# Experts' tokens by row gathers from HBM instead of selection matmuls, in a one-core hybrid layer with a mixture of experts

## Chip, cores and metric

The kernel runs on one core of a Trainium2 chip. The metric is the device time of one execution in microseconds (us).

## What is computed

One layer over 512 latent tokens of width 1024: modulated RMSNorm, two parallel branches (retention and a gated long convolution) merged and projected by `w_out`, a gated residual, and then the part that matters here: a second modulated RMSNorm, a two-level router and 32 SwiGLU experts, of which each token takes two.

```python
x = x + gt1 * mix                                  # mix ends with "@ w_out"
h2 = rms_norm(x, norm2_g) * (1 + sc2) + sh2        # u, the experts' input
group_p = softmax(u @ rg_w + rg_b)                 # 4 groups, the best one
in_group = (u @ re_w + re_b) of that group         # 8 experts, the best two
weights = p_star * w_top / sum(w_top)
for each expert e: y = (silu(x_e @ w1[e]) * (x_e @ w3[e])) @ w2[e]   # x_e: the tokens that chose e
x = x + gt2 * (sum over a token's two experts of weight * y)
return rms_norm(x, final_norm_g)
```

Everything is fp32. An expert has 6.3 MB of weights, all experts together 201.3 MB, and each is read once.

## The kernel before, in words

The first half of the program (up to about 548 us) computes the two branches and their merge; the change leaves it as it is. Behind it come four stages.

*W_out* (`out_group`, `fm_products`, line 1279 on). The product with `w_out` is made feature-major: for each of two halves, eight k-steps of twelve matmuls (weight and activation are each split into a high and a low fp32r part, `mm3`). `out_tile` (line 1236) turns each of eight finished 128x512 tiles into the residual `xm` by one DVE instruction, and makes two copies of it: `xa`, scaled by the modulation `am2c` (1 + sc2 times the norm's gain), and `sq2`, its square.

*Router* (`router_step`, `tail`, lines 1252 to 1340). For each of the eight feature tiles one matmul of `rw` against `xa` and one of ones against `sq2` run over all 512 tokens as moving columns. The result `rl` lies feature-major and is turned to token-major by way of `rsum`. Four of the eight steps run between the steps of the second half of W_out, four behind them. Meanwhile `xa` is turned to token-major, split into `h2H` and `h2L`, and kept in SBUF. After the norm's scale `mrs` come two rounds of a top search (`top`, line 1370), and `pos` (line 1403): for each token and each of 32 experts the token's place in the expert's list (1 to 64, or 0).

*Choice of the experts' tokens* (`select_steps`, line 1444). Four experts make a group, two a pair, and each expert has 64 slots (`CAP`). For a group, DVE builds the 0/1 matrix `gtm` (512 tokens by 256 slots) by comparing `slots` with `pos`. PE then makes the experts' columns `xgm` (features by slots) by multiplying: for each of eight feature tiles, 4 token tiles by two parts of `h2`, so 64 matmuls of 256 columns (lines 1466 and 1467). Another eight (`rss`, line 1457) bring the norm's scale to the slots; DVE multiplies by it, ACT adds the shift `sh2c`.

*Experts* (loop at line 1629). For a pair: `up_half` (16 + 16 matmuls by w1 and w3, two experts side by side in the array), `hidden` (SiLU, product), `turned` (four PE transposes), `down` (by w2), and `add`, which scatters the results back to the tokens by the turned choice `cmb` and adds them to `xmid`, the token-major residual. `spread` (line 1474) makes `cmb` and the slots' weights `wsl`. PE's order is as written in the loop (`manual_schedule` for PE); the stage from `tail` to the first expert's columns is written out for all engines; elsewhere the scheduler orders.

*Weights.* 192 tiles of 1 MB (`plan`, line 1168) come over SP's DMA queue in the order in which they are used, issued ahead by `ahead` (line 1211). Tiles live in a ring of `NR` = 10 places; beside it, places are lent (`loans`, line 1190): for four tiles at the start those of `y`, `cmb`, `hh` and `hT`, later two in every 13 tiles those of `xm` and one (`XE`) those of `xe0` and `xe1`. A tile is issued only when its place is free. The pool `wk`, in which the lent places lie, overlays the tiles of the first half (`wide`), `xa`, `sq2` and W_out's operands among them. One overflow branch (`OV` = pair 10) treats experts with more than 64 tokens; with these inputs it isn't entered.

```python
1465            for t in range(4):
1466                T.matmul(p, h2[0][:, t, ks], gt[:, t], start=(t == 0), stop=False)
1467                T.matmul(p, h2[1][:, t, ks], gt[:, t], start=False, stop=(t == 3))
1468            x_ = x4[:, k % 4]
1469            V.tensor_tensor(out=x_, in0=p, in1=rss, op=ALU.mult)
1470            A.activation(x_, x_, AF.Identity, bias=sh2c[:, k:k + 1])
```

Of the kernel before, what the change touches and what calls it, by code (L numbers as in the profile page):

```python
# [31 lines left out]
NA, NB, NC, NR, NW, NH = 12, 33, 4, 10, 2, 3  # L32
# [5 lines left out]
XE = 8  # L38
# [10 lines left out]
W = 4, 2, 1, 6, 2  # L49
# [124 lines left out]
def body(es: ExitStack, tc: tile.TileContext, d, out, dump=None):  # L174
# [890 lines left out]
    def rest_of_modulation():  # L1065
# [37 lines left out]
        V.scalar_tensor_tensor(out=am2c, in0=am2c, scalar=1.0, in1=n2, op0=ALU.add, op1=ALU.mult)  # L1103
        yield
# [58 lines left out]
    h2 = [r2.tile([128, 4, 1024], F32R, name="h2%s" % n) for n in "HL"]  # L1163
# [18 lines left out]
    def borrow(pool, tag, bufs, units):  # L1182
        def tile_():
# [13 lines left out]
                 if (i - early_tiles) % (NR + 3) < 2 and not 12 * OV + 8 <= i < 12 * OV + 8 + OA + 8)  # L1197
    loans.update((i, [borrow(wk_, "xe0", 1, 2), borrow(lambda: late, "xe1", 1, 2)]) for i in range(early_tiles, len(plan) - 4)
                 if (i - early_tiles) % (NR + 3) == XE)
# [33 lines left out]
    xa, sq2 = [None] * 8, [None] * 8  # L1233
    rl = []

    def out_tile(o, k):
        xk = xm[k // 2][:, k % 2, :]
        V.scalar_tensor_tensor(out=xk, in0=o, scalar=gt1c[:, k:k + 1], in1=xk, op0=ALU.mult, op1=ALU.add)
        if k % 2 == 0:
            xw = wide("xa", (128, 2, 512))  # L1240
            sw = wide("sq2", (128, 2, 512))
            xa[k], xa[k + 1], sq2[k], sq2[k + 1] = xw[:, 0, :], xw[:, 1, :], sw[:, 0, :], sw[:, 1, :]
        if k >= 4 and k % 2:
            V.tensor_scalar(out=xa[k], in0=xk, scalar1=am2c[:, k:k + 1], scalar2=None, op0=ALU.mult)
        else:
            A.activation(xa[k], xk, AF.Copy, scale=am2c[:, k:k + 1])
        A.activation(sq2[k], xk, AF.Square)
# [9 lines left out]
    def turned_tokens(t, n, tag):  # L1257

        p = bank("h2t", tag)
        for q in range(4):  # L1260
            T.transpose(p[:, 128 * q:128 * q + 128], xa[4 * n + q][:, 128 * t:128 * t + 128], ident)
        return [h[:, t, 512 * n:512 * n + 512] for h in h2] + [p]

    def early_steps():
        rl.append(bank("rl"))
        yield
        for k in range(4):
            router_step(k)
            yield
        for t in range(4):  # L1270
            split(*turned_tokens(t, 0, "x"))
            yield
# [25 lines left out]

    tri, ones_b = (rk(n, [128, 128], dt=BF16) for n in ("tri", "ones_b"))
# [8 lines left out]

    def tail():

        for m in range(4):
# [4 lines left out]
            if m > 1:  # L1316
                router_step(2 + m)
        router_step(6)
        router_step(7)
        early_table(AF.Sqrt, sq2[7][:, 0:1])  # L1320
        tk = [turned_tokens(t, 1, "acc") for t in range(2)]
        rsum = wide("rsum")[0:96, 0:512]
        V.tensor_copy(rsum, rl[0][0:96])
        A.copy(tk[0][0], tk[0][2])
        p = bank("lt")
        for t in range(4):
            T.transpose(p[:, 96 * t:96 * t + 96], rsum[:, 128 * t:128 * t + 128], ident[0:96, 0:96])
        pv = p[:, 0:384].rearrange("p (t e) -> p t e", t=4)
        tk += [turned_tokens(t, 1, "acc") for t in range(2, 4)]

        def low(t):
            V.tensor_tensor(out=tk[t][1], in0=tk[t][2], in1=f(tk[t][0]), op=ALU.subtract)

        rsqrt_mean(mrs, pv[:, :, 64], 1024, mtmp, mss)
        for t in range(1, 4):
            A.copy(tk[t][0], tk[t][2])
        V.tensor_tensor(out=lgt, in0=pv[:, :, 0:40], in1=mrs[:, :, None].to_broadcast([128, 4, 40]), op=ALU.mult)
        V.tensor_tensor(out=lgt, in0=lgt, in1=lconst[:, None, :].to_broadcast([128, 4, 40]), op=ALU.add)
        dump("lgt", lgt)
        return tk, low  # L1340
# [3 lines left out]
    tk, low = tail()  # L1344

# [4 lines left out]
    rsb = wk.tile([128, 2, 4], F32R, name="rsb")  # L1350
    xmid = wk.tile([128, 4, 1024], F32, name="xmid")

    def residual():
        for t in range(4):
            for n in range(2):
                p = bank("xmt")
                for q in range(4):
                    k = 4 * n + q
                    T.transpose(p[:, 128 * q:128 * q + 128], xm[k // 2][:, k % 2, 128 * t:128 * t + 128], ident)
                A.copy(xmid[:, t, 512 * n:512 * n + 512], p)  # L1360
                if t == 1 and n:
                    A.copy(rsb[:, 0], mrs)
            dump("xm_%d" % t, xmid[:, t, :])

    def b8(t):
        return t[:, :, :, None].to_broadcast([128, 4, 5, 8])

# [12 lines left out]
    residual()  # L1380
# [18 lines left out]
    V.tensor_tensor(out=rsb[:, 1], in0=mrs, in1=f(rsb[:, 0]), op=ALU.subtract)  # L1399
    low(0)  # L1400
# [6 lines left out]
    def shares():  # L1407
# [7 lines left out]
        for u, oh in ((v1, oh1), (v2, oh2)):  # L1415
            V.tensor_tensor(out=oh, in0=oh, in1=e, op=ALU.mult)
            V.tensor_reduce(out=u, in_=oh, axis=AX.X, op=ALU.add)
        gw = rk("gw", [128, 4, 4])
# [9 lines left out]
        A.copy(wHL[:, :, :, 0, :], wtv)  # L1428
        V.tensor_tensor(out=wHL[:, :, :, 1, :], in0=wtv, in1=f(wHL[:, :, :, 0, :]), op=ALU.subtract)
# [9 lines left out]

# [364 lines left out]
```

## Time and profile before

| | |
|---|---|
| time, median of 3 runs (lowest to highest) | 1124.71 us (1123.62 to 1126.41) |
| the profiled execution: time, span | 1124.28 us, 1122.6 us |
| busy: PE, DVE, ACT, POOL | 98%, 52%, 31%, 2% |
| moved by DMA | 283.22 MB, mean 252 GB/s |
| of it SP's queue, POOL's queue | 274.51 MB, 7.80 MB |
| first expert product (start) | 625.63 us |

The time is that of the whole execution, the span runs from the first to the last instruction on the core; 1.7 us lie around it. Busy shares are means over stages with different limits, and a matmul that waits in the pipeline counts as busy, so the stages are read one by one. In the rows, L12 is line 12 of the kernel before; engines are PE (matmul), PEld (its weight load), DVE, ACT, POOL, SP; a name with q is an engine's queue, on which DMAs are issued.

### The profile page before, as it was taken

How to read it: one execution, taken by the hardware profiler on the slowest of the kernel's cores; microseconds unless marked ns; L12 is line 12 of the kernel's file. 1: busy time of each engine (PE TensorE's matmuls, PEld its weight loads, DVE VectorE, ACT ScalarE, POOL GpSimd, SP SyncE). 2: the span in 40 equal slices, each digit the busy share in tenths (PEclk: the TensorE clock that was granted, in tenths of full speed). 3: DMA queues.
4: the chain of work that ended last, by engine and by line, in shares of the span. 5: the costliest groups of instructions: out<-in, count | busy, mean ns of one | idle time of the engine just before them, and what ended most of it. 6: DMA issues, size and time to landing. Idle time of an engine off the chain costs nothing. (4 is left out here: it accounts for less than half of the span.)

```text
span 1122.6 us, 13708 instructions
## 1 busy us (share of the span) xinstructions
PE 1100.6 (98%) x5338; PEld 710.5 (63%) x5338; DVE 582.1 (52%) x1041; ACT 349.4 (31%) x620; POOL 18.6 (2%) x41
## 2 busy tenths in 40 slices
PE   6999999999999999999999999999999999999996
PEld 3667888877778777877865644454545454645443
DVE  1788995765475768965524523333333323332333
ACT  2487352435533554333234311020202010201113
POOL 0010000000000000000000000000000000000000
PEclk8999999999999999999999999999999999999999
DMA  7653343211122118874392978999999998999992
GB/s 271 209 172 109 112 136 126 75 57 57 57 86 64 57 38 286 263 265 160 129 415 94 398 303 358 417 416 418 415 418 416 419 417 350 399 415 417 418 381 76
DMA packets 63135, 283.22 MB, mean 252 GB/s; under 512 B 6806, under 2 KB 8982, under 8 KB 44506
## 3 DMA queue, kind: packets, MB, share of 16 engines
q1 hardware_dynamic: 60970, 274.51, 64.2%
q0 software_dynamic: 2096, 7.80, 2.1%
q8 instruction: 43, 0.70, 0.3%
q14 instruction: 26, 0.21, 0.1%
HBM read 280.18 MB, written 2.10 MB: 251 GB/s over the span
## 5 line engine op out<-in xcount | busy, mean ns | idle before, releaser
L198 DVE TENSOR_TENSOR wL<-raw,wH 128x512 fp32r<-128x512 f32 x142 | 97.2, 688 | 120.0 <-ACT wH L197 111.3
L197 ACT CAST wH<-raw 128x512 fp32r<-128x512 f32 x142 | 88.1, 621 | 213.3 <-PE ro L202 33.7
L1498 PE MATMUL ga<-ew,xgm 128*64 128x512 f32 x416 | 108.2, 593 | 0.0
L1504 DVE TENSOR_TENSOR hh<-hh,up 128x512 f32<-128x512 f32 x16 | 11.0, 688 | 176.4 <-PE up L1498 176.4
L1498 PE MATMUL up<-ew,xgm 128*64 128x512 f32 x376 | 100.9, 592 | 0.0
L1523 PE MATMUL y<-ew,hT 128*64 128x512 f32 x368 | 97.7, 606 | 1.6 <-DVE hT L1512 1.1
L197 ACT CAST yh<-yv 128x512 fp32r<-128x512 f32 x30 | 18.5, 618 | 200.5 <-DVE yv L1529 187.1
L1498 PEld LDWEIGHTS ga<-ew,xgm 128*64 128x64 f32 x416 | 34.3, 137 | 57.9 <-issue 54.9
L1498 PEld LDWEIGHTS up<-ew,xgm 128*64 128x64 f32 x376 | 31.9, 137 | 54.3 <-issue 52.9
L1523 PEld LDWEIGHTS y<-ew,hT 128*64 128x64 f32 x368 | 30.1, 139 | 48.2 <-issue 46.2
L1466 PE MATMUL xg<-gtm,h2H 128*128 128x256 f32 x256 | 60.5, 280 | 0.0
L1467 PE MATMUL xg<-gtm,h2L 128*128 128x256 f32 x256 | 59.8, 278 | 0.0
L1529 DVE SCALAR_TENSOR_TENSOR yv<-y,wsl,gt 128x512 f32<-128x512 f32 x30 | 22.4, 748 | 62.2 <-PE y L1523 53.1
L1503 ACT ACTIVATE hh<-ga 128x512 f32<-128x512 f32 x16 | 9.6, 597 | 132.2 <-PE ga L1498 129.9
L1466 PEld LDWEIGHTS xg<-gtm,h2H 128*128 128x128 f32 x256 | 48.1, 188 | 0.8 <-issue 0.8
L1467 PEld LDWEIGHTS xg<-gtm,h2L 128*128 128x128 f32 x256 | 48.1, 188 | 0.0
L1546 DVE TENSOR_TENSOR xmid<-xmid,co 128x512 f32<-128x512 f32 x58 | 39.8, 687 | 12.5 <-PE co L1538 11.9
L1538 PE MATMUL co<-yh,cmb 128*128 128x512 f32 x114 | 46.1, 404 | 0.0
L1469 DVE TENSOR_TENSOR xgm<-xg,rss 128x256 f32<-128x256 f32 x64 | 27.0, 424 | 35.3 <-PE xg L1467 35.3
L1538 PE MATMUL co<-yl,cmb 128*128 128x512 f32 x114 | 44.7, 392 | 0.0
L1470 ACT ACTIVATE xgm<-xgm,sh2c 128x256 f32<-128x256 f32 x64 | 32.4, 509 | 35.7 <-DVE xgm L1469 35.7
L342 DVE SCALAR_TENSOR_TENSOR acc<-adaw,scT,acc 128x1024 f32<-128x1024 f32 x28 | 35.6, 1282 | 10.8 <-DMA adaw<-ada 10.7
(478 smaller groups left out, 2383.7 us busy)
## 6 DMA issues: line engine op xcount, KB each, us to landing
ew<-w SPq DMA_DIRECT2D x148, 1024.0 KB, 13.2
raw<-w_in SPq DMA_DIRECT2D x52, 512.0 KB, 3.9
xwxm<-w SPq DMA_DIRECT2D x52, 512.0 KB, 15.0
adaw<-ada SPq DMA_DIRECT2D x32, 512.0 KB, 5.9
xwxe<-w SPq DMA_DIRECT2D x26, 512.0 KB, 16.5
adaw<-ada SPq DMA_DIRECT2D x32, 256.0 KB, 6.2
raw<-ret_w_o SPq DMA_DIRECT2D x8, 512.0 KB, 3.7
raw<-w_out SPq DMA_DIRECT2D x8, 512.0 KB, 4.0
```

The costliest lines, as they stand in the source:

```text
L197: A.copy(h, src)
L198: V.tensor_tensor(out=l, in0=src, in1=f(h), op=ALU.subtract)
L342: V.scalar_tensor_tensor(out=acc[i], in0=w, scalar=scT[:, k, 0:1], in1=acc[i], op0=ALU.mult, op1=ALU.add)
L1466: T.matmul(p, h2[0][:, t, ks], gt[:, t], start=(t == 0), stop=False)
L1467: T.matmul(p, h2[1][:, t, ks], gt[:, t], start=False, stop=(t == 3))
L1469: V.tensor_tensor(out=x_, in0=p, in1=rss, op=ALU.mult)
L1470: A.activation(x_, x_, AF.Identity, bias=sh2c[:, k:k + 1])
L1498: T.matmul(ab_[i][64 * e:64 * e + 64], xg[k][:, c0 + 64 * e:c0 + 64 * e + 64], w[e][q], start=(k == 0), stop=(k == 7))
L1523: T.matmul(y_[n][64 * e:64 * e + 64], hT_[:, 128 * k + 64 * e:128 * k + 64 * e + 64], w[e][2 * q + n], start=(k == 0), stop=(k == 3))
L1529: V.scalar_tensor_tensor(out=yv, in0=y_[n], scalar=wsl, in1=gt2[:, ns], op0=ALU.mult, op1=ALU.mult)
L1538: T.matmul(p, cmb[:, 128 * t:128 * t + 128], y[j][:, ns], start=(start and i + j == 0), stop=(i == len(parts) - 1 and j == 1))
L1546: V.tensor_tensor(out=xmid[:, t, ns], in0=xmid[:, t, ns], in1=p, op=ALU.add)
```

## The change

The experts' columns are no longer made by a product with the choice. Each token's residual row is copied to HBM (`rows`, 512 x 1024) by eight POOL DMAs as soon as it is turned to token-major. For a pair of experts the matmul that gave the slots' weights (`slot_sums`) now also sums, for each slot, the norm's scale (two parts) and the token's number minus 1024. `fetched` adds 1024 to that sum, which gives an index, and issues an indirect DMA on POOL's queue that reads row `idx` of `rows` into the slot's partition of `xr`; an empty slot's index is 1024, beyond the bound of 511. `scaled` multiplies the row by the norm's scale (half on DVE, half on ACT), `token_columns` turns it by eight PE transposes, and DVE and ACT apply `am2c` and `sh2c` as they move the turned columns to `xgm`. `xr` has one buffer for each pair of a group.

The modulation goes into the router's weights (`rw` times `am2c`), so `xa` and `h2` are gone. The router is token-major: `xm` is the stationary side and 40 columns of `rw` move, so no turn of its result is needed; it runs in three partial sums. The squares are added up on DVE and summed by eight one-column products. `xmid` is made in the router's stage rather than by `residual` behind it. The ring has 12 places rather than 10, and `xf` is one more place to lend. In the expert loop, the choice of the next group is made during the group's first pair, and `described` (slot sums, gathers, weights, turned choice) stands behind `add` and ahead of the first pair's `down`.

```diff
-NA, NB, NC, NR, NW, NH = 12, 33, 4, 10, 2, 3
+NA, NB, NC, NR, NW, NH = 12, 33, 4, 12, 2, 3
-XE = 8
+XE, XF = 8, 12
-W = 4, 2, 1, 6, 2
+W = 4, 2, 1, 10, 2, 8
...
+        V.tensor_tensor(out=rw, in0=rw, in1=am2c[:, :, None].to_broadcast([128, 8, 64]), op=ALU.mult)
...
+    loans.update((i, [borrow(wk_, "xf", 1, 4)]) for i in range(early_tiles, len(plan) - 4)
+                 if (i - early_tiles) % (NR + 4) == XF)
...
-    def router_step(k):
-
-        T.matmul(rl[0][0:64], rw[:, k, :], xa[k], start=(k == 0), stop=(k == 7))
-        T.matmul(rl[0][64:96], ones[:, 0:32], sq2[k], start=(k == 0), stop=(k == 7))
+    def router_part(ks, t):
+        p = rl[-1][:, 40 * t:40 * t + 40]
+        for k in ks:
+            T.matmul(p, xk_tile(k, t), rw[:, k, 0:40], start=(k == ks[0]), stop=(k == ks[-1]))
...
+    def kept(t, n, p):
+        ns = slice(512 * n, 512 * n + 512)
+        A.copy(xmid[:, t, ns], p)
+        G.dma_start(rows[128 * t:128 * t + 128, ns], xmid[:, t, ns])
...
-    def select_steps(pos, n, name, res, slots, tag="xg", bufs=2):
...
+    def slot_sums(gt, c0, whl):
+        p = bank("wsl")
+        n = whl.shape[-1]
         for t in range(4):
+            T.matmul(p[:, 8 - n:8], gt[:, t, c0:c0 + 128], whl[:, t], start=(t == 0), stop=(t == 3))
+        return p
+
+    def fetched(p, j):
+
+        idx = wk.tile([128, 1], I32, name="idx", tag="idx", bufs=2)
+        rs = wk.tile([128, 1], F32, name="rs", tag="rs", bufs=2)
+        V.tensor_scalar(out=idx, in0=p[:, 6:7], scalar1=1024.0, scalar2=None, op0=ALU.add)
+        G.indirect_dma_start(out=xr[j], out_offset=None, in_=rows,
+                             in_offset=bass.IndirectOffsetOnAxis(ap=idx, axis=0), bounds_check=511, oob_is_err=False)
+        V.tensor_reduce(out=rs, in_=p[:, 4:6], axis=AX.X, op=ALU.add)
+        return rs
+
+    def scaled(rs, j):
+        V.tensor_scalar(out=xr[j][:, 0:512], in0=xr[j][:, 0:512], scalar1=rs, scalar2=None, op0=ALU.mult)
+        A.activation(xr[j][:, 512:1024], xr[j][:, 512:1024], AF.Copy, scale=rs)
...
+            for j, pr in enumerate(pairs):
+                T.transpose(p[:, i + 128 * j:i + 128 * j + 128], xr[pr][:, 128 * k:128 * k + 128], ident)
...
+            if k % 2:
+                A.activation(o, p[:, i:i + w], AF.Identity, bias=sh2c[:, k:k + 1], scale=am2c[:, k:k + 1])
+            else:
+                V.tensor_scalar(out=o, in0=p[:, i:i + w], scalar1=am2c[:, k:k + 1], scalar2=sh2c[:, k:k + 1],
+                                op0=ALU.mult, op1=ALU.add)
...
+            if g < 7:
+                nxt = described(g + 1, gt)
...
-        hh = up(a + 1, sel[1])
+        hh = up(a + 1, xg)
         if g < 7:
-            some(more, 3)
+            for j in range(2):
+                scaled(rs[j], j)
             hT_ = turned(hh)
-            run(more)
-            spr = [spread(nxt[0], 128 * j, weights_of(a + 2 + j)) for j in range(2)]
+            xg = column_tiles(4, "m")
+            token_columns(xg, [0, 1])
             parts.append((now[1][0], down(hT_, now[1][1], ahead_weights)))
```

The order in which the instructions stand shows three places. The first is SP's queue from the last load of `w_out` on, where the weight tiles are issued ahead (`ew` is the ring; `xwy`, `xwcmb`, `xwxm`, `xwxe` and `xwxf` are lent places, and four rows of 128x512 or two of 128x1024 make one tile). Before:

```order
L484 DMA raw<-w_out 128x1024
L1225 DMA ew<-w 128x2048 x5
L1207 DMA xwy<-w 128x1024 x4
L1207 DMA xwcmb<-w 128x512 x4
L1207 DMA xwhh<-w 128x512 x2
L1207 DMA xwhT<-w 128x512 x2
```

The changed kernel, at the same place (the lines are those of its own text):

```order
L484 DMA raw<-w_out 128x1024
L1230 DMA ew<-w 128x2048 x7
L1212 DMA xwy<-w 128x1024 x4
L1212 DMA xwcmb<-w 128x512 x4
L1212 DMA xwhh<-w 128x512 x2
L1212 DMA xwhT<-w 128x512 x2
L1212 DMA xwxm<-w 128x1024 x4
L1212 DMA xwxe_5353<-w 128x1024
L1212 DMA xwxf<-w 128x2048
```

Two more ring tiles stand ahead of the first lent place, and a lent tile `xwxf` is new; the order of the rest is kept.

The second place is POOL's queue from the start of the expert stage's constants to the second group. Before, it holds a broadcast only:

```order
L830 TENSOR_TENSOR sq<-sq 128x512 x3
L1307 IOTA slots 128x64
L1607 ISA
L1607 ISA gt_5263<-mrow_70 128x512 x2
L1560 TENSOR_LOAD nrounds
L1561 COMPARE_AND_BRANCH
```

The changed kernel:

```order
L1322 IOTA slots 128x64
L1273 DMA rows<-xmid 128x512 x8
L1376 MEMSET xr_5098 128x1024
L1376 MEMSET xr_5099 128x1024
L1483 DMA xr_5098<-rows,idx 128x1024
L1483 DMA xr_5099<-rows,idx 128x1024
L1648 ISA
L1648 ISA gt_5274<-mrow_70 128x512 x2
```

The row copies and the clearing of `xr` stand ahead of the first two gathers, and the broadcast of `gt2` behind them; later groups have two gathers each.

The third place is DVE in a middle group of the changed kernel, from the four additions to `xmid` that end a group's first pair to its first `yv`. Before, `yv` followed the additions directly:

```order
L1546 TENSOR_TENSOR xmid<-xmid,co 128x512 x4
L1512 COPY hT<-hT 128x512
L1546 TENSOR_TENSOR xmid<-xmid,co 128x512 x4
L1529 SCALAR_TENSOR_TENSOR yv<-y,wsl,gt_5263 128x512
L198 TENSOR_TENSOR yl<-yv,yh 128x512
L1529 SCALAR_TENSOR_TENSOR yv<-y,wsl,gt_5263 128x512
L198 TENSOR_TENSOR yl<-yv,yh 128x512
```

The changed kernel:

```order
L1582 TENSOR_TENSOR xmid<-xmid,co 128x512 x4
L1482 TENSOR_SCALAR idx<-wsl 128x1
L1485 TENSOR_REDUCE rs<-wsl 128x1
L1524 TENSOR_REDUCE wsl<-wsl 64x1 x2
L1517 CAST cmb<-cmb 128x512
...
L1466 TENSOR_TENSOR gtm<-slots,pos 128x4x128 x2
L1489 TENSOR_SCALAR xr_5098<-xr_5098,rs 128x512
L1489 TENSOR_SCALAR xr_5099<-xr_5099,rs 128x512
L1565 SCALAR_TENSOR_TENSOR yv<-y,wsl,gt_5274 128x512
```

The two scalings of `xr`, which need the gathered rows, now stand ahead of `yv` on DVE.

## Rows read from the trace of the kernel before

**Rows 1.** The page: the span, and each engine's busy time, share and instructions.
```profile
span 1122.6 us, 13708 instructions
...
PE 1100.6 (98%) x5338; PEld 710.5 (63%) x5338; DVE 582.1 (52%) x1041; ACT 349.4 (31%) x620; POOL 18.6 (2%) x41
```

**Rows 2.** Windows: stretch, length, busy per engine, PE clock, DMA share, GB/s.
```profile
595.00:613.00 18.00, 18.00 (x81) 9.64 (x80) 8.26 (x15) 8.67 (x16) 1.48 (x2) 1.00 0.00 1
613.00:650.00 37.00, 35.90 (x235) 23.29 (x235) 21.50 (x66) 12.86 (x25) 0.00 (x0) 0.96 0.95 369
650.00:690.00 40.00, 40.00 (x228) 20.18 (x226) 13.63 (x28) 7.52 (x14) 0.00 (x0) 0.99 0.81 310
690.00:925.00 235.00, 235.00 (x1258) 120.16 (x1256) 77.44 (x144) 31.24 (x58) 0.00 (x0) 1.00 1.02 417
925.00:965.00 40.00, 39.48 (x184) 17.65 (x182) 13.93 (x23) 3.07 (x5) 0.00 (x0) 1.00 0.92 357
...
1095.00:1112.00 17.00, 17.00 (x67) 8.40 (x66) 5.03 (x11) 4.10 (x12) 0.00 (x0) 1.00 0.00 1
```

**Rows 3.** SP's timeline (start, length) and its waits (total, times, longest us).
```profile
574.31 2.35 SPq L1225 DMA_DIRECT2D ew<-w  x5
612.89 1.75 SPq L1207 DMA_DIRECT2D xwy<-w  x4
...
SPq L1207 <- DVE xa L1244: 29.8, 1, 29.8
```

**Rows 4.** The chain that ended last, one group: start, us, engine, instructions.
```profile
949.72 7.13 PE y L1523 x32
...
970.58 1.13 PE rss L1457 x8
971.71 0.12 PE xg L1466
...
973.60 0.44 PE hT L1510 x4
...
979.70 0.44 PE cmb L1479 x4
...
1010.05 7.02 PE y L1523 x32
```

**Rows 5.** PE's timeline: a router step, W_out's last product, the first expert product.
```profile
575.35 1.07 PE L1254 MATMUL rl<-xa,rw 128*64 128x512 f32 x2
...
577.33 0.50 PE L201 MATMUL wo<-mixed,wH 128*128 128x512 f32 x1
...
604.26 0.40 PE L203 MATMUL wo<-mixed,wL 128*128 128x512 f32 x1
...
625.63 3.65 PE L1498 MATMUL ga<-ew,xgm 128*64 128x512 f32 x16
```

**Rows 6.** DMA: a queue's share of 16 engines; issues (count, KB each, us to landing).
```profile
q0 software_dynamic: 2096, 7.80, 2.1%
...
ci<-dft_i POOLq DMA_DIRECT2D x4, 512.0 KB, 3.7
...
xwxe<-w SPq DMA_DIRECT2D x26, 512.0 KB, 16.5
```

**Rows 7.** DVE's timeline: the first search of the router, and `pos`.
```profile
613.94 0.32 DVE L1373 TENSOR_REDUCE t1v<-lgt 128x20 f32<-128x160 f32 x1
...
619.55 0.29 DVE L1403 SCALAR_TENSOR_TENSOR pos<-cum,asg 128x128 f32<-128x128 f32 x1 [0.39 <-PE cum L1398]
```

**Rows 8.** PE's timeline: the first pair's y products behind an idle microsecond.
```profile
647.20 5.35 PE L1523 MATMUL y<-ew,hT 128*64 128x512 f32 x16 [1.08 <-DVE hT L1512]
652.38 3.60 PE L1523 MATMUL y<-xwy,hT 128*64 128x512 f32 x16
```

**Rows 9.** The chain that ended last: the last up products.
```profile
1087.42 3.43 PE up L1498 x16
```

More of the change, by code (lines that the diff above doesn't have):

```diff
@@ L1328, in tail @@
[L1328 to L1337, printed above, removed]
+            if m == 0:
+                V.tensor_copy(lgt_v, rl[0][:, 0:160])
@@ L1348, in body @@
     t1.close()
     wk = es.enter_context(tc.tile_pool(name="wk", bufs=1, side="left", reuse_waits="tile"))
[L1350 to L1363, printed above, removed]
+    wHL = wk.tile([128, 4, 16, 8], F32R, name="wHL")
@@ L1365, in b8, with b16 @@
+    xr = [wk.tile([128, 1024], F32, name="xr%d" % i) for i in range(2)]
+    for x_ in xr:
+        G.memset(x_, 0.0)
+    nrounds = wk.tile([128, 1], I32, name="nrounds")
     def b8(t):
         return t[:, :, :, None].to_broadcast([128, 4, 5, 8])
+    def b16(t):
+        return t[:, :, None].to_broadcast([128, 4, 16])
+    A.copy(wHL[:, :, :, 4], b16(mrs))
+    for c in (6, 7):
+        A.copy(wHL[:, :, :, c], b16(tok))
     lv = lgt.rearrange("p t (s e) -> p t s e", e=8)
@@ L1474, in spread, with chosen @@
-    def spread(gt, c0, whl):
-        cs = slice(c0, c0 + 128)
+        yield
+    def chosen(gt, pos, n, slots, parts=1):
+        w = n // parts
+        for i in range(parts):
+            V.tensor_tensor(out=gt[:, :, w * CAP * i:w * CAP * (i + 1)].rearrange("p t (e s) -> p t e s", s=CAP),
+                            in0=slots[:, None, None, :].to_broadcast([128, 4, w, CAP]),
+                            in1=pos[:, :, w * i:w * i + w, None].to_broadcast([128, 4, w, CAP]), op=ALU.is_equal)
+            yield
@@ L1593, in some, with rows_of @@
             next(gen, None)
-    sel = []
-    more = chosen(0, sel)
-    some(more, 3)
-    low(1)
-    low(2)
-    low(3)
-    some(more, 3)
+    def rows_of(g):
+        gt = wk.tile([128, 4, 4 * CAP], F32R, name="gtm", tag="gt", bufs=1)
+        return gt, chosen(gt, pos[:, :, 4 * g:4 * g + 4], 4, slots, 2)
+    gt, more = rows_of(0)
+    xg = column_tiles(4, "m")
+    rs = []
+    for j in range(2):
+        next(more)
+        rs.append(fetched(slot_sums(gt, 128 * j, wHL[:, :, j, 4:8]), j))
+    weights_ = shares()
+    next(weights_)
+    keep_warm(W[5])
+    scaled(rs[0], 0)
+    token_columns(xg, [0])
     ahead(early_tiles + 2)
@@ L1644, in body @@
             ahead(early_tiles + 14)
-            up_half(ab_, 1, sel[1], 0, ahead_weights)
+            up_half(ab_, 1, xg, 0, ahead_weights)
             hh = hidden(ab_)
-            spr = [spread(sel[0], 128 * j, weights_of(j)) for j in range(2)]
+            now = []
+            for j in range(2):
+                wsl = slot_weights(slot_sums(gt, 128 * j, wHL[:, :, j]))
+                now.append((turned_choice(gt, 128 * j), wsl))
             hT_ = turned(hh)
+            rs = []
         else:
-            hh = up(a, sel[1])
+            now = nxt
+            if g < 7:
+                gt, more = rows_of(g + 1)
+                run(more)
+            hh = up(a, xg)
             add(parts, places[:4])
```

208 lines of the change are left out of this document (109 added, 99 removed).

## The prediction

> **What bounds the kernel now.** I read the page's engine line first: PE is busy for 98% of the span, and the other engines for half of it or less [rows 1]. A busy PE can still be a PE that follows something else, so the second view is the table of stretches with the DMA rate [rows 2]. The reader is to see two things there. From 690 to 925 us the DMA engines run at 417 GB/s without a break, so that is the ceiling of this traffic here. Around it stand holes: nothing at all from 595 to 613, 369 and 310 GB/s up to 690, 357 GB/s from 925 to 965. The third view, the queue's own timeline and waits, says why the first hole is there: the last of the ten ring tiles is issued at 574.31 + 2.35, the next tile, lent from the place of `xa`, at 612.89, and that issue waited 29.8 us for `xa` [rows 3].
>
> The experts' weights are 192 tiles of 1.049 MB. One tile takes 1.049 / 417 = 2.51 us, a group of four experts (24 tiles) 60.3 us. The fourth view, the chain, gives PE's side of a group: from 949.72 to 1010.05, 60.3 us too [rows 4]. So PE and DMA are level in the expert stage, and a gain on PE alone is worth only what it lets the DMA stream close of its holes. **The sum is therefore made on the DMA stream:** where it stands idle, what bytes are added, and what follows its last landing.
>
> **The change, part by part.**
>
> *PE in a group.* The `rss` products (1.13 us) and 64 selection products go; the latter lie between 971.71 and 979.7 with a 0.44 us turn inside, so 7.5 us. Added are 16 turns, priced by the four `hT` turns in 0.44 us: 1.8 us [rows 4]. A group falls from 60.3 to 53.4 us. Worth nothing by itself: the stream needs 60.3 us and more. DVE and ACT lose a pass each over the gathered columns and gain a scaling; both are at half load or less [rows 1] and the scaling lies under up products that need neither, so I cost that at nothing; without that cover it would be under 1 us a group.
>
> *The router.* A step of the feature-major router occupies PE from 575.35 to 577.33, 1.98 us [rows 5], and five of the eight stand before the last product of W_out. They become 16 products of 40 columns, at a turn's 0.11 us 1.8 us, plus four turns moved ahead, 0.4 us. So W_out ends 9.9 - 2.2 = 7.7 us earlier, at 604.66 - 7.7 = 597.0 [rows 5]. From there to the first expert product it took 21.0 us (625.63). Now, counted from 597.0: residual 0.8, four products 0.4, sums of squares 0.9, root and scaling 2.0, and a little of waits, 4.8 in all; the two top-k's to `pos`, from 613.94 to 619.84 in the old order, 5.9 [rows 7]; first half of the choice 0.7, slot sums and index 0.7; the gather; scaling and the first turned columns 1.7. That is 13.8 us and the gather.
>
> *The gather's time.* No row shows an indirect DMA. The nearest are a 512 KB load on POOL's queue, 3.7 us from issue to landing while the engines had room, and a 512 KB loan on SP's full queue, 16.5 us [rows 6]. The gather also waits for the eight row copies, which precede it on POOL's queue with two memsets, while the loans are in flight. I take 6.5 us: nearer the POOL row, since it has a queue of its own, but with company. The first product then stands at 597.0 + 20.3 = 617.3. The Trainium skill (DMA: Bandwidth & Descriptors, Queues, rings and completion order) says that an engine takes turns between the queues it has work for, packet by packet. By that rule the gather doesn't stand behind the megabytes on SP's queue and lands near the POOL row, with the sum below; without it, like the loan, with the time of the late gather among the rivals. No run here shows both queues loaded at once.
>
> *The hole from 595 to 613.* Two more ring tiles (5.0 us) and the first four row copies (1.05 MB, 2.5 us) carry the stream to 602.5; the loans' places held W_out's operands and the squares, free by about 599. So the hole closes: **-18.0 us.**
>
> *From 613 to 690.* The loss there is 37 x (1 - 369/417) + 40 x (1 - 310/417) = 14.5 us [rows 2]. The loans, now with a whole-tile place more (7.5 tiles, 18.8 us), and the other four row copies (2.5 us) last to 623.8, and the first two tiles come free at 617.3 + 3.4 = 620.7. Later the buffers are three tiles (7.5 us) deeper and PE frees them faster. What stays lies between 0 and 14.5; I keep 5, since the queue is issued in order and single places still come free late: **-9.5 us.**
>
> *From 925 to 965.* Loss 40 x (1 - 357/417) = 5.8 us [rows 2]. With 18 tiles in hand at the first product, PE eating 24 in 53.4 us and the stream bringing 24 in 61.9 (below), the lead is gone after about 290 us, near 910. From there PE waits for tiles and places are free; I keep 0.5: **-5.3 us.**
>
> *Bytes.* The copy of the residual is 2.10 MB, 5.0 us at 417 GB/s. The gathers move 1024 assigned rows of 4 KB, 4.19 MB. POOL's queue took 2.1% of the engines' span for 7.80 MB, which is 331 GB/s [rows 6]; so 12.7 us. Bounds: 10.0 us at 417 GB/s, and 25.3 us if the empty slots' rows are moved as well (2048 rows). Sum: **+17.7 us.** A group then takes the stream 60.3 + 1.6 = 61.9 us.
>
> *The end.* The stream ends at 1095 and the span 27.6 us later [rows 1, 2]; there PE was behind, its last up product ending at 1087.42 + 3.43 [rows 9], 31.7 us before the end. If PE waits for weights, the last up tile lands four tiles (10.0 us) ahead of the stream's end, 3.4 us of products follow, then the same 31.7 us: 25.1 us. **-2.5 us.**
>
> *The added wait.* In every later group DVE waits for the gather before it scales `xr`, and the first pair's `yv` is queued behind. Their PSUM banks are wanted again only after y (7.0 us) and the next up products (13.7 us), so a gather under 20 us stays hidden; the longest landing of a comparable size is 16.5 [rows 6].
>
> Sum: -18.0 - 9.5 - 5.3 + 17.7 - 2.5 = -17.6 us. The profiled execution took 1124.28 us, so **1106.7**; it stands 0.4 us below the median of the runs, which is within what they differ by. I forecast 1107 us.
>
> **The rivals.**
>
> *A late first gather.* If it lands like a loan, in 16.5 us, the first product moves to 627.3, the first places come free at 630.7, and the stream stands still for 6.9 us: 1113.6. For it: the row copies must have landed first, beside full traffic.
>
> *PE's clock becomes the bound late.* Before the y products at 647.20 PE stood idle 1.08 us, the granted clock fell to its half level, and 16 of them took 5.35 us where the next 16 took 3.60 [rows 8]: 1.75 us lost. From 910 on PE will wait in every group, 8.5 us in sum. Five such losses a group use that up. A PE that is late doesn't wait, so it catches itself; I price it at 5 us of work left over at the end: 1112. The Trainium skill (TensorE: Matmul & The Clock Gate, Part 1: The HAM clock gate) has the slow clock as the idle state, which activity lifts; by that rule the losses come whenever PE starves. The row agrees.
>
> *Empty slots are moved too.* +12.6 us: 1119. Against it: their index lies outside the bound that the call gives.
>
> *Slower: the gather holds the engines.* If many 4 KB rows from scattered places keep all 16 engines from the weights for longer than their bytes need (0.8 us a gather), 16 gathers pay it in a stage that has no slack. It decides the sign from (17.6 + 3.4) / 16 = 1.3 us more, 2.1 us a gather; at 3 us each it is 35 us: 1142. Against it speak the 331 GB/s of POOL's rows.
>
> *The hole only moves.* If the chain to the first product takes 38 us rather than 20, the stream stands still for 14 us where it now stands 18: 1121, no change. For it: the chain gains a round trip through HBM.
>
> **How the numbers follow.** A measurement of this kernel tells 0.3% (3.4 us) from no change. Forecast 0.60; late gather 0.12; clock 0.08; empty slots 0.08; hole moves 0.04; gather holds engines 0.08. Faster: 0.60 + 0.12 + 0.08 + 0.08 = 0.88; same 0.04; slower 0.08. The range reaches up to the empty slots, 1120. Down it takes the gathers at 417 GB/s (-2.7), no loss kept between 613 and 690 (-5.0) and row copies that fall in holes (-5.0): 1094.
>
> **What would show it.** Right: the first expert product near 617; 400 GB/s or more from 597 to the end, no hole over 3 us; PE idle from about 900 on, its waits ended by `ew` tiles; a group taking 62 us; about 6.3 MB more moved. Wrong: PE still never waiting; a hole of 10 us between 600 and 640 (late gather); a group of 65 us with POOL's queue holding much more than 2% of the engines (slots or held engines); a PE clock well under full after 900 with no waits for DMA.

## The result, and the profile after

The changed kernel takes 1141.22 us in the median (1139.54 to 1147.66), against 1124.86 us before: a ratio of 1.0155, 95% interval 1.0114 to 1.0197. It is slower by 16 us where I forecast a gain of 17.6. The profiled execution took 1140.63 us.

The page, its span and engine lines, and POOL's queue (packets, MB, share of 16 engines):

```profile
span 1138.9 us, 13047 instructions
...
PE 1077.3 (95%) x4958; PEld 675.8 (59%) x4958; DVE 579.5 (51%) x1045; ACT 337.9 (30%) x588; POOL 41.1 (4%) x68
...
q0 software_dynamic: 5040, 14.10, 3.6%
```

PE has less work than before [rows 1], as forecast, and POOL's queue moved 14.10 MB where it had moved 7.80 [rows 6]. The 6.3 MB more are the copy of the residual and the 1024 assigned rows; empty slots weren't moved.

The stretches of [rows 2], in the same columns:

```profile
595.00:613.00 18.00, 17.72 (x129) 16.68 (x129) 11.72 (x33) 8.02 (x15) 4.01 (x7) 0.91 1.03 411
613.00:650.00 37.00, 26.69 (x107) 14.69 (x107) 10.92 (x37) 6.92 (x13) 3.63 (x4) 0.72 0.64 253
650.00:690.00 40.00, 35.14 (x180) 14.74 (x178) 14.74 (x34) 6.13 (x10) 2.24 (x2) 0.97 0.80 300
690.00:925.00 235.00, 222.31 (x1036) 94.82 (x1032) 76.32 (x145) 27.20 (x44) 7.92 (x8) 0.96 1.00 412
925.00:965.00 40.00, 35.63 (x158) 16.60 (x159) 13.74 (x23) 4.09 (x7) 0.00 (x0) 0.91 0.91 364
```

The hole from 595 to 613 is closed (411 GB/s for 1). But another has opened behind it (253 for 369), the two others are as they were (300 for 310, 364 for 357), and for the first time PE's busy time and its clock are below full in the middle of the stage. So the reader's next view is what PE waits for in the expert stage (total us, times, longest):

```profile
PE xg L1500 <- DVE xgm L1505: 23.1, 33, 1.0
PE hT L1546 <- DVE hh L1540: 6.6, 7, 1.2
PE wsl L1475 <- DVEq L1597: 1.4, 1, 1.4
PE xg L1500 <- ACT xgm L1503: 1.1, 2, 0.5
PE y L1559 <- DVE hT L1548: 1.0, 1, 1.0
```

That is all of it: 33 us, and not one wait for a weight. PE is the bound from its first expert product to the end, not the DMA stream. The first expert product starts at 632.38 us (625.63 before, 617.3 forecast), and the chain that ended last puts the last up products here (start, us):

```profile
1103.58 3.43 PE up L1534 x16
```

They end at 1107.01. So the first product is 6.75 us later than before, the stretch from it to the last up products is 474.6 us for 465.2, and what follows is as long as it was (31.9 us for 31.8). 6.75 + 9.4 + 0.1 is the 16.3 us by which the span has grown.

PE's timeline shows where a group loses its time. Here are the second pair's turns of a group (start, us, instruction, idle time before and what ended it):

```profile
743.86 0.66 PE L1546 MATMUL hT<-ident,hh 128*128 128x128 f32 x4 [0.89 <-DVE hh L1540]
744.35 0.38 PE L1500 MATMUL xg<-ident,xr 128*128 128x128 f32 x2
745.75 0.66 PE L1500 MATMUL xg<-ident,xr 128*128 128x128 f32 x4 [1.02 <-DVE xgm L1505]
747.04 0.66 PE L1500 MATMUL xg<-ident,xr 128*128 128x128 f32 x4 [0.64 <-DVE xgm L1505]
748.34 0.72 PE L1500 MATMUL xg<-ident,xr 128*128 128x128 f32 x4 [0.64 <-DVE xgm L1505]
749.70 0.69 PE L1500 MATMUL xg<-ident,xr 128*128 128x128 f32 x2 [0.64 <-DVE xgm L1505]
750.32 1.12 PE L1559 MATMUL y<-xwxf,hT 128*64 128x512 f32 x1
```

Between two batches of turns PE waits for the eviction of a column that lies in the same PSUM bank. From 744.35 to 750.32 this takes 6.0 us, where I had 1.8. And the y products behind it begin with records of 1.12 us where 0.59 is usual: after the waits the granted clock stands at its half level (0.50 from 750.4 to 755.4, which is 1.2 GHz for 2.4). That stretch and two whole groups, by windows:

```profile
750.40:755.40 5.00, 5.00 (x12) 1.40 (x14) 0.00 (x0) 0.56 (x1) 0.00 (x0) 0.50 1.02 421
743.90:805.10 61.20, 57.41 (x264) 24.39 (x264) 20.09 (x38) 7.36 (x12) 1.98 (x2) 0.94 1.02 416
805.10:863.80 58.70, 54.50 (x265) 23.88 (x265) 20.09 (x38) 7.36 (x12) 1.98 (x2) 1.00 1.02 416
```

The same work takes 61.2 us at a mean clock of 0.94 and 58.7 at 1.00. Both are far above my 53.4. Of the six whole groups from 682.6 to 1048.7, five run at a mean clock of 0.94 or 0.95.

### The profile page after: what moved, and what is told of

Same layout as the page of the kernel before. It is cut to its first block, busy times and chain, and to the rows that moved or that the text cites. A ratio compares the mean times of both kernels' runs of the same rounds, so it can differ in the third digit from the quotient of the medians.

```text
span 1138.9 us, 13047 instructions
## 1 busy us (share of the span) xinstructions
PE 1077.3 (95%) x4958; PEld 675.8 (59%) x4958; DVE 579.5 (51%) x1045; ACT 337.9 (30%) x588; POOL 41.1 (4%) x68
## 3 DMA queue, kind: packets, MB, share of 16 engines
q1 hardware_dynamic: 59818, 274.51, 62.9%
q0 software_dynamic: 5040, 14.10, 3.6%
## 5 line engine op out<-in xcount | busy, mean ns | idle before, releaser
L1534 PE MATMUL up<-ew,xgm 128*64 128x512 f32 x496 | 111.7, 592 | 0.0
L1559 PE MATMUL y<-ew,hT 128*64 128x512 f32 x368 | 105.2, 653 | 1.0 <-DVE hT L1548 1.0
L1534 PE MATMUL ga<-ew,xgm 128*64 128x512 f32 x280 | 93.4, 619 | 0.0
L1500 PE MATMUL xg<-ident,xr 128*128 128x128 f32 x128 | 29.5, 339 | 29.5 <-DVE xgm L1505 24.6
L1490 ACT ACTIVATE xr<-xr,rs 128x512 f32<-128x512 f32 x16 | 11.5, 722 | 152.5 <-DMA xr<-rows,idx 152.5
L197 ACT CAST yh<-yv 128x512 fp32r<-128x512 f32 x30 | 18.5, 618 | 104.2 <-DVE yv L1565 92.5
L1582 DVE TENSOR_TENSOR xmid<-xmid,co 128x512 f32<-128x512 f32 x58 | 39.8, 688 | 12.5 <-PE co L1574 11.9
L1534 PEld LDWEIGHTS ga<-ew,xgm 128*64 128x64 f32 x280 | 28.4, 144 | 24.0 <-issue 24.0
L1503 ACT ACTIVATE xgm<-xg,sh2c,am2c 128x256 f32<-128x256 f32 (+1 forms) x36 | 19.4, 540 | 77.7 <-PE xg L1500 77.7
L1500 PEld LDWEIGHTS xg<-ident,xr 128*128 128x128 f32 x128 | 16.3, 160 | 41.3 <-DVE xgm L1505 34.4
L1489 DVE TENSOR_SCALAR xr<-xr,rs 128x512 f32<-128x512 f32 x16 | 7.8, 486 | 60.9 <-DMA xr<-rows,idx 60.9
L1505 DVE TENSOR_SCALAR xgm<-xg,am2c,sh2c 128x256 f32<-128x256 f32 (+1 forms) x36 | 18.4, 512 | 32.8 <-PE xg L1500 32.8
```

Source lines behind the costliest of these rows:

```text
L197: A.copy(h, src)
L1490: A.activation(xr[j][:, 512:1024], xr[j][:, 512:1024], AF.Copy, scale=rs)
L1500: T.transpose(p[:, i + 128 * j:i + 128 * j + 128], xr[pr][:, 128 * k:128 * k + 128], ident)
L1503: A.activation(o, p[:, i:i + w], AF.Identity, bias=sh2c[:, k:k + 1], scale=am2c[:, k:k + 1])
L1505: V.tensor_scalar(out=o, in0=p[:, i:i + w], scalar1=am2c[:, k:k + 1], scalar2=sh2c[:, k:k + 1], op0=ALU.mult, op1=ALU.add)
L1534: T.matmul(ab_[i][64 * e:64 * e + 64], xg[k][:, c0 + 64 * e:c0 + 64 * e + 64], w[e][q], start=(k == 0), stop=(k == 7))
```

## Experiments

Theory A: PE is the bound in the expert stage, because the turns and the evictions of a bank take turns, and because PE's clock falls behind these waits; the late first product comes on top. Theory B, the rival whose time (1142 us) the result seems to confirm: the stream is the bound, since gathers hold the DMA engines. Each time stands against the kernel before, run on the same chip.

**Turns by bank.** All turns of a bank before its first eviction:

```diff
-            for j, pr in enumerate(pairs):
-                T.transpose(p[:, i + 128 * j:i + 128 * j + 128], xr[pr][:, 128 * k:128 * k + 128], ident)
+                for q in range(k, k + 512 // w):
+                    for j, pr in enumerate(pairs):
+                        c = w * q % 512 + 128 * j
+                        T.transpose(p[:, c:c + 128], xr[pr][:, 128 * q:128 * q + 128], ident)
```

> Edit of the changed kernel: all turns that fill one PSUM bank are issued before its first eviction, so that a turn no longer stands behind the eviction of the column next to it in the same bank. Theory A (PE's chain in a group is the bound: turns and evictions take turns, 0.64 us of waiting each time, and PE's clock falls behind them): a group of 60.9 us falls to 56 to 57.5, the waits of the turns from 23 us in the expert stage to under 8, first product 3 us earlier; time 1115 to 1124 us, with the DMA stream as the next bound. Theory B (the DMA stream is the bound, because the gathers take the engines): a faster PE gives nothing, 1137 to 1142 us.

1118.23 us, ratio 0.9939 (0.9921 to 0.9957): 23 us less than the changed kernel, from an order of instructions alone, and faster than before. A group's turns now, on PE's timeline:

```profile
726.99 0.65 PE L1548 MATMUL hT<-ident,hh 128*128 128x128 f32 x4 [0.89 <-DVE hh L1542]
727.48 1.91 PE L1502 MATMUL xg<-ident,xr 128*128 128x128 f32 x16
729.32 0.64 PE L1561 MATMUL y<-xwxf,hT 128*64 128x512 f32 x1
...
781.47 0.66 PE L1548 MATMUL hT<-ident,hh 128*128 128x128 f32 x4 [0.89 <-DVE hh L1542]
```

Sixteen records without a wait in 1.84 us to the next product, the 1.8 of the forecast, and y at full clock. From this `hT` to that of the next group it is 54.5 us, where I had 53.4. PE's waits in the stage:

```profile
PE up L1536 <- DMA ew<-w: 12.7, 12, 1.5
PE hT L1548 <- DVE hh L1542: 6.5, 7, 1.2
PE ga L1536 <- DMA ew<-w: 5.8, 6, 1.3
```

Now PE does wait for weights (18.5 us, 15.7 of it behind 860 us), as the forecast had it, and groups late in the stage take 61.8 and 62.5 us (836.31 to 898.09, 963.39 to 1025.86; forecast 61.9). The first product stands at 629.41. This is theory A. That the stream is the next bound is tested below (bank, one gather).

**One gather.** Of the gathers only the first group's two are kept.

```diff
-    def fetched(p, j):
+    def fetched(p, j, first=True):
...
+        if first:
+            G.indirect_dma_start(out=xr[j], out_offset=None, in_=rows,
...
-            rs.append(fetched(p, j))
+            rs.append(fetched(p, j, False))
```

> Edit of the changed kernel: the gathers of the second to eighth group are left out (the first group's rows are scaled and turned again in their place), so 14 of 16 gathers, some 3.7 MB, are not moved. Theory A (PE's chain is the bound): no change against the changed kernel within 3 us, 1138 to 1144 us, a group still 60 to 61 us. Theory B (gathers hold the DMA engines): their bytes alone are 14/16 of 12.7 us, 11 us, and more if they hold engines: 1130 us or less, a group shorter by 1.6 us or more.

1148.59 us (1.0215, 1.0196 to 1.0234): no gain from moving 3.7 MB less. That excludes theory B. PE waits as in the changed kernel:

```profile
PE xg L1501 <- DVE xgm L1506: 23.1, 33, 1.0
```

That its median is 7 us slower I had not expected. Its profiled execution is 5.0 us longer than that of the changed kernel, and a single group, the one with the overflow branch, is 5.4 us longer (68.3 us from 923.95 to 992.26, for 62.9). In it PE stands idle for 2.2 us in which the profile shows nothing that it waits for, and the y products behind that take 9.24 us for 7.09. Why PE stands idle there wasn't tried.

**Warm between.** Is it the waits or the clock? Products of ones fill the waits, and the order of the turns stays.

```diff
+        fill = bank("warm")
...
+            if len(pairs) > 1 and k % 2 == 0:
+                for _ in range(4):
+                    T.matmul(fill[:, 0:128], ones, ones, start=True, stop=True)
```

> Edit of the changed kernel, turns as they are: four products of ones with ones stand between a group's turns, in each stretch in which PE waits for the eviction, and take no longer than the wait. Theory A has two parts, 4.1 us of waits a group and up to 2.4 us in the groups where PE's clock falls to its half level behind them. With PE kept active the clock stays full and only the waits are left: a group 58 to 59 us in place of 60.9, 1124 to 1131 us. If the slow clock costs nothing or doesn't come from the waits: 1138 us or more.

1130.50 us (1.0053, 1.0034 to 1.0072). The work added is useless, and the kernel gains 10.7 us over the changed one. The clock from 690 to 860 us, in the changed kernel and in this one:

```profile
690.00:860.00 170.00, 162.36 (x762) 69.61 (x760) 56.80 (x108) 19.84 (x32) 5.94 (x6) 0.97 1.00 409
```

```profile
690.00:860.00 170.00, 166.74 (x843) 77.30 (x841) 57.49 (x109) 20.39 (x33) 5.93 (x6) 1.00 1.02 416
```

A group takes 58.4 us (742.35 to 800.77), and from `hT` to the first y product it is still 6.25 us. The time between turns stayed about as it was, and the clock changed. So of the 23 us that the turns by bank gain, about 10.7 are the clock's. The remaining 12.3 come with the waits themselves, the earlier first product among them, less what PE then waits for weights.

**Turns inside.** The turns by bank, moreover spread: half behind the third block of up products, a quarter on each side of `hT`.

```diff
...
+        hh = up(a + 1, xg, first_columns if g < 7 else None)
...
+            token_columns(xg, [0, 1], 0, range(4, 6))
             hT_ = turned(hh)
+            token_columns(xg, [0, 1], 0, range(6, 8))
```

> Edit of the changed kernel: as the turns by bank, and beyond that the first half of the columns is turned behind the third block of up products of a group's second pair, a quarter ahead of hT and a quarter behind it, so that they cover the waits for hh and hT. Theory A: PE's idle time in a group falls under 1 us, its clock stays full, a group would take 54 us of PE; then PE waits for weights late in the stage, and the time is the DMA stream's: 1112 to 1120 us, no slower than the turns by bank. Theory B: 1137 to 1142 us.

1118.54 us (0.9946, 0.9929 to 0.9963): no different from the turns by bank. The waits for `hh` fall from 6.5 us to 2.0, but those of y for `hT` rise from 1.0 to 3.5, and those for weights from 18.5 to 19.8. While tiles are in stock a group takes 54.8 us (672.24 to 727.04), no less than the 54.5 of the turns by bank. So PE won no time here, and the run doesn't test what a faster PE would give.

**Bank, one gather.** The same cut as in one gather, now on the turns by bank.

> Edit of the turns by bank: the gathers of groups two to eight are left out (14 of 16; the first rows stay in place). Here PE waits for weights late, so the stream's bytes should count. By the forecast's price (331 GB/s) 14 gathers of 262 KB are 11 us, at 417 GB/s 9 us: 1107 to 1110 us. If gathers hold the engines beyond their bytes: under 1105 us. If PE is still the bound: 1115 us or more.

1109.82 us (0.9863, 0.9843 to 0.9883): 8.4 us less for 14 gathers, 0.60 us each; 3.7 MB at 417 GB/s are 8.8. The two intervals leave the 8.4 uncertain by about 3 us. So once the stream is the bound, a gather costs about its bytes, far from the 2.1 us at which the rival would have decided the sign; where PE is the bound, leaving them out gained nothing (one gather).

**Bank, ring of 10.**

```diff
-NA, NB, NC, NR, NW, NH = 12, 33, 4, 12, 2, 3
+NA, NB, NC, NR, NW, NH = 12, 33, 4, 10, 2, 3
...
-    loans.update((i, [borrow(wk_, "xf", 1, 4)]) for i in range(early_tiles, len(plan) - 4)
-                 if (i - early_tiles) % (NR + 4) == XF)
```

> Edit of the turns by bank: ring of 10 tiles as before the change, and without the whole-tile place, so 3 tiles (7.5 us of stream) fewer are loaded ahead of the first product. If the longer ring is what fills the old hole: the stream stops 7.5 us earlier, the hole behind it grows by as much, 1124 to 1129 us. If PE's chain or the end were the bound: 1118 to 1120 us.

1124.28 us (0.9993, 0.9979 to 1.0007), the time before the change. The three tiles are worth 6.1 us of the 7.5 that they take to load, although without them the first product comes 4.0 us sooner (625.37). Without them the rest of the change, turns mended, brings nothing. Whether three more tiles alone would have helped the kernel before wasn't tried.

**Loans held**, on the changed kernel: SP copies the second index to HBM ahead of the last loans, so that these wait for it.

```diff
...
+    ahead(early_tiles)
+    S.dma_start(mark, held_idx[1])
     ahead(early_tiles + 2)
```

> Edit of the changed kernel: ahead of the loans from the place of xm SP issues a 512-byte copy of the second index, so that the last three and a half tiles of the prefetch are issued behind the first gathers' indices. Theory C (the first gather lands late because it shares the engines with the loans): it lands within 5 us of its issue instead of 8, the first product comes 3 to 5 us earlier (628 instead of 632), PE's chain behind it keeps its length, and the time falls by 3 to 5 us: 1136 to 1138 us. If the gather's time is its own (descriptors, rows, the copies ahead of it), the first product stays at 632 or later and the time at 1140 us or above.

1144.41 us (1.0158, 1.0125 to 1.0190), and no verdict on the theory, since the window behind the copy's issue (616.28) shows a disturbance:

```profile
617.00:629.00 12.00, 2.73 (x25) 2.54 (x23) 2.07 (x7) 0.00 (x0) 2.08 (x2) 0.71 0.82 67
```

The engines count as 82% busy and move 67 GB/s, and the gather's rows are used at 633.35. The copy has 128 rows of 4 bytes. In the next run, without a copy, the same window moved 287 GB/s at 84%. What the copy does in the engines no run shows.

**Bank, loans held** does the same without a transfer of its own, by letting DVE read `xm` behind the index.

```diff
+    for i in range(4):
+        V.tensor_copy(junk1, xm[i][:, 0, 0:1])
     weights_ = shares()
```

> Edit of the turns by bank: DVE reads one column of xm behind the second index, so that the loans from the places of xm, and the two issued behind them, wait for the index without a transfer of their own. Theory C (the first gather lands late because it shares the engines with these loans): row copies and gather land sooner, the gather within 5 us of its issue instead of 8, first product 624 to 626 us instead of 629.4; the stream stands still for 2 to 4 us before and as much less behind: 1114 to 1119 us. If the gather's time is its own: first product at 629 us or later, 1118 to 1123 us.

1117.98 us (0.9935, 0.9914 to 0.9956), as the turns by bank. From the gather's issue to DVE's first use of the rows it is 6.6 us (617.54 to 624.10; I had expected 5) where it was 8.05 (618.90 to 626.95); in the ring of 10, where the queue ran dry at this time, it is 4.3 (619.35 to 623.64). The engines moved 246, 367 and 131 GB/s meanwhile. So in full company the gather takes about twice as long. The first product comes at 626.55 and the time stays; the loans from `xm` are issued 7.0 us later (617.97 for 610.99).

**First by products**, on the turns by bank: the first group's columns come by 32 products of `xmid` with the choice (times the norm's factor), without gathers.

```diff
+                T.matmul(o_, xmid[:, t, 128 * k:128 * k + 128], gts[:, t], start=(t == 0), stop=(t == 3))
...
-            token_columns(xg, [1], 128)
+            chosen_columns(xg, gts, range(4, 8))
```

> Edit of the turns by bank: the first group's columns come without gathers, by 32 products of the residual in SBUF with the choice, which carries the norm's factor; half of them stand behind the first up products; later groups gather as before. Theory A with a late start (what the turns by bank still lose against the forecast is the hole before the first places come free): first product at 621 to 624 us instead of 629.4, the stretch without weights before 640 us shorter by 5 to 8 us, 1 MB less on the engines: 1107 to 1112 us. If the late start were free, because the stream is bound elsewhere: 1116 us or more.

1116.83 us (0.9922, 0.9902 to 0.9943). The first product did come at 623.38, but the gain is 1.4 us, under the 6 expected. The second half of the products takes 7.2 us of PE's path behind the first up products, so the first `hT` comes hardly earlier (646.42 for 647.09). I take from this that places are freed by PE's progress, not by its first product.

**Half by products**: only columns 0 to 3 by products, in time in which PE waits anyway; the others by gathers. **Half kept warm**: twelve products of ones ahead of them (the last line below, which only this run has).

```diff
+    chosen_columns(xg, gts, range(4))
+            token_columns(xg, [0, 1], 0, range(4, 8))
...
         rs.append(fetched(slot_sums(gt, 128 * j, wHL[:, :, j, 4:8]), j))
+        keep_warm(2 + 2 * j)
```

> Edit of the turns by bank: only the first group's columns 0 to 3 come by products of the residual in SBUF with the choice (7.1 us, in time in which PE otherwise warms itself or waits), columns 4 to 7 by the gathers, turned behind the first up products, so nothing long stands on PE's path behind the first product. If PE's path from W_out to the first group's end sets when places come free: first product 622 to 624 us, first hT at 640 to 642 us instead of 647, time 1110 to 1114 us. If the gathers land behind 631 us or the hole is set by something else: 1116 to 1119 us.

> Edit of the half by products: 4 products of ones behind the first slot sums and 8 behind the second, so that PE isn't idle ahead of the 32 records of the choice, which took 9.96 us at half the clock there instead of 7.07. If the clock was what kept the half by products at 627.3 us for its first product: first product at 624 to 625 us, time 2 to 3 us less, 1112 to 1114 us. If other things hold the places: 1115 to 1117 us.

1115.66 us (0.9906, 0.9883 to 0.9929) and 1115.20 us (0.9908, 0.9891 to 0.9924). PE's timeline of the first shows why the first product is late there (627.29):

```profile
617.40 9.96 PE L1516 MATMUL xg<-xgm,xmid 128*128 128x256 f32 x32 [0.67 <-DVE xgm L1661]
```

and of the second, kept warm:

```profile
619.02 7.07 PE L1516 MATMUL xg<-xgm,xmid 128*128 128x256 f32 x32
```

The clock is 0.71 in the first and 1.00 in the second. Kept active, PE does the same products in 7.07 us; but the products of ones delayed their start by 1.6 us, and the first product won 1.3 us, the time nothing that can be told. Both missed the gain that I expected: the first lies between its two ranges, the second in the range for other things holding the places. Of the kernels that leave nothing out they have the lowest medians, 0.9% below the kernel before; the intervals don't tell them from first by products.

**Bank, no branch**: the hole from 925 to 965 us, which the forecast closed, stands in the kernels before and after and in the turns by bank. SP's waits in this stretch, of the turns by bank:

```profile
SPq L1599 <- SPq L1599: 20.1, 4, 12.0
```

Line 1599 is the overflow branch, and SP waits there for itself.

```diff
-GENERAL = True
+GENERAL = False
```

> Edit of the turns by bank: the code for experts with more than 64 tokens (a branch that all engines pass in the sixth group, not entered with these inputs) is left out. The stretch from 925 to 965 us ran at 357 GB/s before the change and at 360 to 364 with it and with the turns by bank, where the forecast had it close. Theory D (SP stands at this branch and issues nothing): the stretch runs at 410 GB/s or more, PE waits less for weights behind it, and the time is 4 to 6 us less, 1112 to 1114 us. If the places of the ring come late there for another reason: the hole stays, 1117 to 1119 us.

1115.00 us (0.9916, 0.9899 to 0.9932), and the stretch, before the edit and with it:

```profile
925.00:965.00 40.00, 37.21 (x173) 17.77 (x170) 15.56 (x32) 3.28 (x5) 1.98 (x2) 0.96 0.89 360
```

```profile
925.00:965.00 40.00, 39.15 (x192) 18.91 (x190) 16.98 (x34) 5.21 (x9) 1.97 (x2) 1.00 1.02 417
```

In this kernel the hole is the branch's. The time falls by 3.2 us, near the least that can be told; a wait of PE's own at the branch, 1.4 us, goes with it. In the kernel before, SP stood at the branch for 7.4 us of the stretch and for 20.4 us waited on y and `ga` products, so there places came late as well.

## Why the prediction was wrong, step by step

**"A group falls from 60.3 to 53.4 us"** is the step that failed. The 16 turns were priced by the four `hT` turns, which share a bank and have one eviction behind all of them; the change's code evicts each column before it turns the next into the same bank. From `hT` to the first y product it took 6.15 us in the full-clock group (805.13 to 811.28), where I had 2.2, and 0.89 us of waiting for `hh` stand ahead, which the selection products used to cover: 53.4 + 3.9 + 0.9 = 58.2, of 58.7 measured. The rest, up to 61.2, is the clock. With the turns by bank 1.84 us take the place of the 6, and a group is 54.5. I asked whether DVE and ACT had room for the evictions (they had), and not whether PE waited for them. The Trainium skill (PSUM — Partial Sum Buffer, PSUM bank collisions raise a hardware error) says that two engines must not be at one bank in the same partitions at once, different columns included, and that the compiler's scheduler therefore makes one instruction depend on the other; by that rule a turn behind an eviction in its bank waits. The traces agree: waits of 0.64 us with the change's order, none with the turns by bank. I hadn't weighed this rule. A bank is also one tile of this program, and whether the wait is kept by bank or by tile no run tells apart.

So "the sum is made on the DMA stream" fell with it: with groups of 61 us PE never waited for a weight, and the terms of the sum were not what set the end.

**The first product**, 617.3 forecast, 632.38 measured. Its stages on PE's timeline:

```profile
599.44 0.39 PE L203 MATMUL wo<-mixed,wL 128*128 128x512 f32 x1
599.67 3.66 PE L1260 MATMUL rl<-rw,xm 128*128 128x40 f32 x32
603.16 1.92 PE L1352 MATMUL ss<-ones,sq 128*128 128x1 f32 x16
...
625.86 0.41 PE L1500 MATMUL xg<-ident,xr 128*128 128x128 f32 x1 [2.77 <-DVE xr L1489]
626.77 0.47 PE L1500 MATMUL xg<-ident,xr 128*128 128x128 f32 x1 [0.51 <-DVE xgm L1505]
...
632.38 5.51 PE L1534 MATMUL ga<-ew,xgm 128*64 128x512 f32 x16
```

and on DVE's, the first index and the first use of the gathered rows:

```profile
614.60 0.16 DVE L1482 TENSOR_SCALAR idx<-wsl 128x1 int32<-128x1 f32 x1 [0.76 <-PE wsl L1475]
...
625.27 0.49 DVE L1489 TENSOR_SCALAR xr<-xr,rs 128x512 f32<-128x512 f32 x1 [5.62 <-DMA xr<-rows,idx]
```

and on POOL's queue, the last row copies and the first gather:

```profile
607.36 1.60 POOL L1273 DMA_DIRECT2D rows<-xmid  x3 [0.32 <-ACT xmid L1272]
...
617.13 1.12 POOL L1483 DMA_INDIRECT xr<-rows,idx  x1 [6.32 <-DVE e L1428]
```

W_out ends 2.8 us later than forecast. It begins 1.6 us later in this execution (549.62 for 548.03), and the 16 router products ahead of its end take 3.2 us, not 1.8: a product of 40 columns is two records and 0.20 to 0.23 us, not a turn's 0.11. (Five router steps stood ahead of it before the change, as the working has it, not the four of the words on the kernel before.) From there to the index it is 2.8 us more than forecast: 3.5 us of router products and 1.8 of sums of squares stand there, where I had 1.3 in all, and only a part of my other pieces lay beside them. From index to rows it is 10.5 us, not 6.5: the issue stands at 617.13, 2.4 us behind the index, and from there it is 8.1, between the 3.7 and the 16.5 of the rows that I had. The 2.4 fit a wait for the row copies: the last is issued at 608.4 and lands 7.7 us later, and the gather is issued 1.0 us behind that. In the turns by bank, bank, loans held and the ring of 10 it is 0.9 to 1.0 us as well, while the index is ready 1.3 to 3.5 us ahead of the issue. Scaling and turning take 7.1 us, not 1.7, for the reason above (with the turns by bank, 2.5). 2.8 + 2.8 + 4.0 + 5.4 = 15.0 of the 15.1 us. The late gather was a rival with a chance of 0.12; its mechanism is right (row copies first, full traffic beside it), at 4.0 of the 10 us that it priced.

**The other terms**, on the turns by bank, where the stream does bound the end. The hole from 595 to 613 closed, as forecast. From 613 to 690 nothing was won where I had priced 9.5 us:

```profile
613.00:650.00 37.00, 29.09 (x178) 17.12 (x178) 16.18 (x52) 7.38 (x14) 4.00 (x5) 0.91 0.78 310
650.00:690.00 40.00, 39.11 (x200) 15.32 (x198) 12.96 (x28) 6.44 (x11) 2.24 (x2) 1.00 0.93 360
```

The stretch loses 37 x (1 - 310/417) + 40 x (1 - 360/417) = 15.0 us, for 14.5 before. Its second part, 650 to 690, lost only about half of what it had, but a new hole stands in the first: from 626 to 635 the engines move 21 GB/s, and SP issues the next tile at 633.80, as the first `ga` products (629.41 + 4.36) end. That is the late first product. From 925 to 965 I took it that places would be free once PE waits; the branch, at which SP stood, I hadn't seen, and 5.5 us were lost for my 0.5. Bytes: 14 gathers cost 8.4 us where my price gives 11.1, and 417 GB/s gives 8.8; the uncertainty of 3 us doesn't exclude either. At 0.60 us each, 16 gathers are 9.6 for 12.7. The three (15.0 for the 5 that I kept, 5.5 for 0.5, 9.6 for 12.7) come to 10.0 + 5.0 - 3.1 = 11.9 us; the turns by bank (1118.23) miss the forecast by 11.5. The added wait of DVE behind the gather stayed hidden, as forecast: from issue to landing the gathers took

```profile
DMA to landing us min/median/max: 3.7/8.2/11.0
```

under the 20 us of cover.

**The rivals.** That the gather holds the engines gave almost the measured time, 1142, by a mechanism that isn't there; one gather and bank, one gather show that, and the agreement is luck. That PE's clock becomes the bound was half right: the losses behind waits came, about 2.5 us in most groups, but from the turns and from the first group on, not from waits for weights late in the stage, which in the turns by bank cost no clock (1.00 from 965 to 1060 us). Of the signs for being wrong, two came true in the changed kernel: "PE still never waiting" for weights and a hole of 10 us (3 GB/s from 626 to 638). A third did in part: the clock behind 900 us was 0.95 with no waits for DMA. One sign for being right came true by luck: groups took near 62 us, but the time was PE's and not the stream's.

## What to carry to other kernels

When an instruction on the bound engine is added in a chain with another engine's (write a bank, evict it, write it again), price the round trip, not the instruction: here 16 turns of 0.11 us were 6 us, and 1.8 again once all writes of a bank stood ahead of its evictions. Ask of removed work what it was covering. And a time that fits a rival is no evidence for its mechanism: take away the suspected cost and see.

## What was not expected of the hardware

Useless products in PE's waits made the kernel 10.7 us faster, since PE's granted clock stayed full. Behind a copy of 128 times 4 bytes to HBM the engines counted as 82% busy at 67 GB/s for 12 us (one run). And the first gather took 4.3 us to its first use beside an emptying queue and 8.1 beside a full one, though the two stand on different queues.
